# The adaLN map of layer 0 in quarters beside the input projection

## The chip, the cores and the metric

The kernel runs on one core of one Trainium2 chip. The metric is the device time of one execution in microseconds (us); less is better. Times of runs are given as medians; the profile comes from one execution of its own.

## What is computed

Two layers of a hybrid diffusion backbone over 512 latent and 256 context tokens of width 1024. Only the start of layer 0 matters here. Each token stream gets a shift and a scale from a linear map of its conditioning vector (adaLN); the tokens are normalised, modulated, and multiplied by one input weight:

```python
mod_l = [m[:, None, :] for m in jnp.split(jax.nn.silu(c) @ w_m + b_m, 6, axis=-1)]
mod_c = jnp.split(jax.nn.silu(c_ctx) @ w_m + b_m, 6, axis=-1)
zl = modulate(rms_norm(hl, norm1_g[layer]), mod_l[0], mod_l[1])
zc = modulate(rms_norm(hc, norm1_g[layer]), mod_c[0], mod_c[1])
...
h = z @ w_in
qa, ka, va, cq, ckv, kr = jnp.split(h, EVEN_SPLITS, axis=-1)
```

The columns of w_in are 512 for the queries qa, 256 for ka and va, and 416 for the latents cq, ckv and kr. The map w_m is 1024 x 6144; shift and scale are its first 2048 columns.

## The kernel before

**Data.** Tokens stand with features on the partitions: the 1024 features are 8 k tiles of 128 (KT = 8), so `x3[:, k, :]` is one k tile of all 768 tokens, latent tokens in 0:512 and context tokens in 512:768. A modulated k tile is kept as a pair `zs[k]` (high and low part, tiles `sl`), and a weight unit as a pair too (tiles `w`, made by `wunit` from a raw tile `raw` that a DMA fills: L119 on ScalarE casts the high part, L120 on VectorE subtracts). A product takes three matmuls, high by high, high by low, low by high (L295, L297, L298 in `proj`).

**The map.** `mod_steps` returns 9 steps: step k loads the rows of k tile k for the columns that are wanted (L152) and multiplies them into one PSUM bank (L154; four groups of columns, each in its own 32 partitions), and the last step copies the bank (L160), transposes it (L163) and adds the bias, which gives `modT`. For layer 0 the shift and scale columns come as two halves, `start[0]` and `start[1]`; half h serves the k tiles 4h to 4h+3 of z. Each half is 16 DMAs of 256 KB.

**Norm.** `rstd_steps` gives three steps for a range of tokens: squares summed over k, `total` (a matmul by ones, L247, a little work on VectorE at L250 and on GpSimd at L251), and `spread` (a matmul that repeats the result over the partitions, L256). `normed(h, gi)` makes the gain and the k tiles of half h for token group gi (0 latent, 1 context): L274 on VectorE, L277 on ScalarE, L278 on VectorE.

**Projection.** `proj` goes through k tiles and, within one, through token blocks of 128. The accumulators of ka and va for the four latent blocks share two PSUM banks (`on`), those of qa for the four latent blocks are four banks (`tw`), those of qa for the two context blocks two more (`on`). The written order is: for each half, ka/va of the latent blocks, qa of the latent blocks, (after half 0: the z of the rest), qa of the context blocks. Then ka/va of the context blocks, then the latents (416 columns).

**What sets the order.** Each engine runs its queue in order. The queue of TensorE (PE) is set by a scheduler, except inside a `manual_schedule` block, where it is the order in which the code stands; before, only the 9 steps of `start[0]` are such a block, and the scheduler is free to move matmuls of the projection ahead of or between those of `start[1]`. The other engines' queues and that of the DMAs (SP) are the scheduler's. Tiles come from pools: 11 tiles `w` of 1024 columns (WT), 4 tiles `raw` (RAWS), 33 tiles `sl` (SLAB), 4 single PSUM banks `on`. What fills a tile of a pool waits until the tile's earlier user has been read for the last time.

## Time and profile before

| | us |
|---|---|
| median of 3 runs | 1602.92 (1601.92 to 1606.02) |
| the profiled execution | 1602.01 |
| its span in the profile | 1600.2 |

The span runs from the first to the last instruction that the profile shows; 1.8 us of the execution lie around it. PE is TensorE's matmuls, PEld its weight loads, DVE VectorE, ACT ScalarE, POOL GpSimd, SP the queue that issues the DMAs. An fp32 matmul of the program stands in the profile as two records (128 records of L154 for the 64 matmuls of the map).

### The profile page before, as it was taken

The numbers are of one execution on the slowest core, as the hardware profiler recorded it, in microseconds if no ns is written. First come the engines' busy times: TensorE is split into PE (matmuls) and PEld (weight loads), VectorE is DVE, ScalarE is ACT, GpSimd is POOL, SyncE is SP. The second block draws the span as 40 slices with busy tenths as digits, with TensorE's granted clock in tenths as the row PEclk, the third lists the DMA queues.
The fourth block names the chain that finished last, engine by engine and source line by source line (L and its number), as shares of the span: only waits on it lengthen the run. The fifth ranks groups of instructions, "written<-read, shape, count | busy, mean of one in ns | idle before, by whom it ended". The sixth has DMA issues, their size and how long they took to land.

```text
span 1600.2 us, 25191 instructions
## 1 busy us (share of the span) xinstructions
PE 1539.1 (96%) x9394; PEld 1290.4 (81%) x9394; DVE 1106.6 (69%) x1955; ACT 806.1 (50%) x1574; POOL 353.0 (22%) x607
## 2 busy tenths in 40 slices
PE   6998999999999999999999999999999799999996
PEld 3786666658888888888888888778779799999986
DVE  4667765575469967865487557866667788877775
ACT  4447876674334233232331324535666767766663
POOL 0146444440011011010100100122324222222213
PEclk9999999999999999999999999999999899999998
DMA  9410014354123523622254211321134677776651
GB/s 314 158 53 27 1 53 159 106 172 164 54 80 112 158 66 122 208 65 66 66 172 145 63 57 45 108 66 40 40 87 99 146 181 172 165 175 161 167 119 65
DMA packets 81068, 179.19 MB, mean 112 GB/s; under 512 B 9393, under 2 KB 23729, under 8 KB 80945
## 3 DMA queue, kind: packets, MB, share of 16 engines
q1 hardware_dynamic: 67408, 152.93, 30.4%
q0 software_dynamic: 13536, 24.65, 9.0%
q8 instruction: 74, 1.21, 0.3%
q14 instruction: 50, 0.40, 0.1%
HBM read 150.80 MB, written 2.10 MB: 96 GB/s over the span
## 4 chain that ended last, share of the span: by engine, by line
PE 86%; DVE 5%; ACT 3%; issue 2%; DMA 2%; POOL 1%; SPq 0%; DVEq 0%; ACTq 0%; POOLq 0%
PE tw L125 9%; PE tw L126 9%; PE tw L127 9%; PE on L125 8%; PE on L126 7%; PE on L127 7%; PE on L621 3%; PE on L613 2%; PE on L1398 2%; PE on L1399 2%; PE on L1400 2%; PE tw L298 2%; PE tw L295 2%; PE tw L297 2%; PE tw L1398 2%
## 5 line engine op out<-in xcount | busy, mean ns | idle before, releaser
L125 PE MATMUL tw<-sl,w 128*128 128x512 f32 (+1 forms) x832 | 281.9, 339 | 0.1
L126 PE MATMUL tw<-sl,w 128*128 128x512 f32 (+1 forms) x832 | 280.9, 338 | 0.0
L127 PE MATMUL tw<-sl,w 128*128 128x512 f32 (+1 forms) x832 | 280.3, 337 | 0.0
L120 DVE TENSOR_TENSOR w<-raw,w 128x1024 fp32r<-128x1024 f32 (+3 forms) x119 | 137.7, 1159 | 139.8 <-PE tw L126 98.9
L119 ACT CAST w<-raw 128x1024 fp32r<-128x1024 f32 (+3 forms) x119 | 117.4, 990 | 175.3 <-PE tw L127 152.7
L125 PEld LDWEIGHTS tw<-sl,w 128*128 128x128 f32 x832 | 157.1, 189 | 27.4 <-issue 3.6
L125 PE MATMUL on<-sl,w 128*128 128x512 f32 (+2 forms) x504 | 174.0, 346 | 0.0
L126 PEld LDWEIGHTS tw<-sl,w 128*128 128x128 f32 x832 | 157.1, 189 | 18.9 <-issue 0.8
L127 PE MATMUL on<-sl,w 128*128 128x512 f32 (+2 forms) x504 | 171.7, 341 | 0.0
L126 PE MATMUL on<-sl,w 128*128 128x512 f32 (+2 forms) x504 | 171.7, 341 | 0.0
L127 PEld LDWEIGHTS tw<-sl,w 128*128 128x128 f32 x832 | 156.8, 188 | 17.7
L945 POOL TENSOR_SCALAR sm<-sm,csum,cw 128x2 f32<-128x2 f32 x44 | 30.3, 690 | 477.4 <-ACT sm L944 477.4
L1398 PE MATMUL on<-sl,w 128*128 128x256 f32 x384 | 109.8, 286 | 11.0 <-ACT sl L1463 9.9
L572 POOL TENSOR_SCALAR sl<-sl,sm 128x768 f32<-128x768 f32 (+2 forms) x96 | 84.7, 883 | 159.8 <-DVE sm L571 137.6
L125 PEld LDWEIGHTS on<-sl,w 128*128 128x128 f32 x504 | 95.6, 190 | 19.3 <-issue 7.3
L1399 PE MATMUL on<-sl,w 128*128 128x256 f32 x384 | 109.3, 285 | 0.0
L1400 PE MATMUL on<-sl,w 128*128 128x256 f32 x384 | 109.1, 284 | 0.0
L127 PEld LDWEIGHTS on<-sl,w 128*128 128x128 f32 x504 | 95.3, 189 | 11.1
L126 PEld LDWEIGHTS on<-sl,w 128*128 128x128 f32 x504 | 95.7, 190 | 9.8 <-DVE sl L132 0.2
L963 DVE SCALAR_TENSOR_TENSOR sl<-sl,cw,sl 128x770 f32<-128x770 f32 x88 | 89.4, 1019 | 19.6 <-ACT sl L960 17.9
L570 ACT ACTIVATE sl<-tw,sm 128x768 f32<-128x768 f32 (+2 forms) x96 | 81.8, 852 | 40.2 <-DVE sm L569 32.9
L569 DVE TENSOR_REDUCE sm<-tw 128x1 f32<-128x768 f32 (+2 forms) x96 | 84.9, 886 | 18.2 <-PE tw L787 12.0
(318 smaller groups left out, 3829.0 us busy)
## 6 DMA issues: line engine op xcount, KB each, us to landing
raw<-in_ffn_up_w_dram SPq DMA_DIRECT2D x88, 512.0 KB, 3.7
mraw<-in_mod_w_dram SPq DMA_DIRECT2D x96, 256.0 KB, 3.6
raw<-in_mod_w_dram SPq DMA_DIRECT2D x32, 512.0 KB, 4.0
w<-sl POOLq DMA_DIRECT2D x62, 256.0 KB, 4.1
rawd<-in_ffn_down_w_dram SPq DMA_DIRECT2D x48, 192.0 KB, 3.6
sl<-in_mod_w_dram SPq DMA_DIRECT2D x32, 256.0 KB, 5.4
raw<-in_ffn_down_w_dram SPq DMA_DIRECT2D x16, 512.0 KB, 3.6
w<-raw POOLq DMA_DIRECT2D x32, 256.0 KB, 4.4
```

Source lines behind the costliest of these rows:

```text
L119: act.copy(out=h, in_=raw)
L120: dve.tensor_tensor(out=l, in0=raw, in1=bc(h), op=ALU.subtract)
L125: pe.matmul(out=ps, lhsT=lh, rhs=rh, start=first, stop=False)
L126: pe.matmul(out=ps, lhsT=lh, rhs=rl, start=False, stop=False)
L127: pe.matmul(out=ps, lhsT=ll, rhs=rh, start=False, stop=last)
L569: dve.tensor_reduce(out=st[:, 0:1], in_=ps, axis=AX.X, op=ALU.max, negate=True)
L570: act.activation(out=p, in_=ps, func=AF.Exp, bias=st[:, 0:1], accum_out=st[:, 1:2])
L572: pool.tensor_scalar(out=p, in0=p, scalar1=st[:, 2:3], scalar2=1.0, op0=ALU.mult, op1=ALU.mult)
L963: dve.scalar_tensor_tensor(out=r[:, 2:end], in0=h[:, 2 + o:end + o], scalar=cw[:, f, t:t + 1], in1=r[:, 2:end], op0=ALU.mult, op1=ALU.add)
L1398: pe.matmul(out=ps, lhsT=h[:, o], rhs=rh, start=(first and k == 0), stop=False, skip_group_check=True)
L1399: pe.matmul(out=ps, lhsT=h[:, o], rhs=rl, start=False, stop=False, skip_group_check=True)
L1400: pe.matmul(out=ps, lhsT=l[:, o], rhs=rh, start=False, stop=(last and k == 3), skip_group_check=True)
```

## The change

The shift and scale columns of the map come in four quarters, `start[0]` to `start[3]`, of two k tiles of z each. A step is still one k tile of the map, with four column groups, now 128 wide instead of 256. A DMA takes two k tiles at a time (`rows=2`): 256 columns of 128 x 2 rows, so 256 KB as before, in runs of 1 KB instead of 2 KB; a quarter is 8 DMAs. A `manual_schedule` block now also holds the projection of the latent tokens: between the matmuls of quarter q (its two k tiles, each ka/va and then qa) stand the steps of quarter q+1, two at a time, and `normed` makes two k tiles at a time. The context norm's `total` and `spread` and the z of all context k tiles come in the last quarter, and qa of the context blocks after all of the latent tokens' projection. The calls of `wunit` move with it: a weight unit is asked for one quarter ahead. The number of matmuls of the projection stays; the map's matmuls are twice as many at half the width.

```diff
--- before.py
+++ after.py
@@ -137,7 +137,8 @@
 
     modT = [cp.tile([128, 2, 48], F32, name=f"modT{l}") for l in range(2)]
 
-    def mod_steps(layer, c0s, w):
+    def mod_steps(layer, c0s, w, rows=1):
+
 
         M = {}
         run = 2
@@ -147,9 +148,14 @@
             if k == 0:
                 M["ps"] = one()
             for i in range(0, 4, run):
-                raw = raw_tile(1024) if run * w > 512 else slab()
-                src = A["mod_w"][layer, k * 128:(k + 1) * 128, c0s[i]:c0s[i] + run * w]
-                nc.sync.dma_start(out=raw[:, :run * w], in_=src)
+                if k % rows == 0:
+                    n = rows * run * w
+                    raw = raw_tile(1024) if n > 512 else slab()
+                    src = A["mod_w"][layer, k * 128:(k + rows) * 128, c0s[i]:c0s[i] + run * w]
+                    nc.sync.dma_start(out=raw[:, :n].rearrange("p (j c) -> p j c", j=rows),
+                                      in_=src.rearrange("(j p) c -> p j c", j=rows))
+                    M[i] = raw[:, :n].rearrange("p (j c) -> p j c", j=rows)
+                raw = M[i][:, k % rows]
                 for g in range(i, i + run):
                     pe.matmul(out=M["ps"][32 * g:32 * g + 32, :w], lhsT=cT[:, k, :],
                               rhs=raw[:, (g - i) * w:(g - i + 1) * w], start=(k == 0), stop=(k == KT - 1))
@@ -308,7 +314,7 @@
     G2 = [LAT + (0,), CX + (1,)]
     G1 = [LAT + (0,)]
     GH = [(0, 256, 0), (256, 512, 0)]
-    start = [mod_steps(0, [512 * h, 512 * h + 256, 1024 + 512 * h, 1280 + 512 * h], 256) for h in range(2)]
+    start = [mod_steps(0, [256 * q, 256 * q + 128, 1024 + 256 * q, 1152 + 256 * q], 128, 2) for q in range(4)]
     ukv, uqa = {}, {}
     rows = [rstd_steps(x3, a, b) for a, b, _ in G2]
     rsb = slab()
@@ -317,6 +323,14 @@
     def spread(gi):
         a, b, _ = G2[gi]
         act.copy(out=rsb[:, a:b], in_=rows[gi][2]()[:, :b - a])
+
+    g1 = cp.tile([128, 2, KT], F32, name="gain1")
+
+    def normed(q, gi):
+        a, b, s = G2[gi]
+        dve.scalar_tensor_tensor(out=g1[:, s, 2 * q:2 * q + 2], in0=modT[0][:, s, 8 + 2 * q:10 + 2 * q], scalar=1.0,
+                                 in1=ng1[:, 2 * q:2 * q + 2], op0=ALU.add, op1=ALU.mult)
+        norm_mod(x3, 0, 0, g1, [G2[gi]], [rsb[:, a:b]], zs, range(2 * q, 2 * q + 2))
 
 
     with tc.manual_schedule(engines={mybir.EngineType.PE}):
@@ -328,24 +342,39 @@
                 spread(0)
             if i == 5:
                 ukv[0] = wunit(A["ev_w_kv"][0], 1024)
-    for u in range(2):
-        uqa[u] = wunit(A["ev_w_qa"][u], 1024)
-    for k in range(KT):
-        nc.sync.dma_start(out=x3[:, k, SEQ:T], in_=A["x_cols"][:, k, SEQ:T])
-    g1 = cp.tile([128, 2, KT], F32, name="gain1")
-
-    def normed(h, gi):
-        a, b, s = G2[gi]
-        dve.scalar_tensor_tensor(out=g1[:, s, 4 * h:4 * h + 4], in0=modT[0][:, s, 8 + 4 * h:12 + 4 * h], scalar=1.0,
-                                 in1=ng1[:, 4 * h:4 * h + 4], op0=ALU.add, op1=ALU.mult)
-        norm_mod(x3, 0, 0, g1, [G2[gi]], [rsb[:, a:b]], zs, range(4 * h, 4 * h + 4))
-    zs = [(slab(F32R), slab(F32R)) for _ in range(KT)]
-    normed(0, 0)
-    rows[1][0]()
-    rows[1][1]()
-    spread(1)
-    for f in start[1]:
-        f()
+                uqa[0] = wunit(A["ev_w_qa"][0], 1024)
+        zs = [(slab(F32R), slab(F32R)) for _ in range(KT)]
+        normed(0, 0)
+        shared = banks(0, 2)
+        accs = [shared[t // 2][:, (t % 2) * 256:(t % 2) * 256 + 256] for t in range(4)]
+        qacc = banks(2, 0)
+        for q in range(4):
+            steps = start[q + 1] if q < 3 else []
+            for i, kk in enumerate((2 * q, 2 * q + 1)):
+                for f in steps[4 * i:4 * i + 2]:
+                    f()
+                proj(accs, zs, ukv, A["ev_w_kv"], 4, 256, range(4), (kk,), True)
+                for f in steps[4 * i + 2:4 * i + 4]:
+                    f()
+                if i == 0 and q < 3:
+                    uqa[q + 1] = wunit(A["ev_w_qa"][q + 1], 1024)
+                    if q == 0:
+                        ukv[1] = wunit(A["ev_w_kv"][1], 1024)
+                    if q == 1:
+                        for k in range(KT):
+                            nc.sync.dma_start(out=x3[:, k, SEQ:T], in_=A["x_cols"][:, k, SEQ:T])
+                        rows[1][0]()
+                if i == 1 and q < 3:
+                    steps[8]()
+                    normed(q + 1, 0)
+                proj(qacc, zs, uqa, A["ev_w_qa"], 2, 512, range(4), (kk,))
+                if i == 0 and q == 3:
+                    rows[1][1]()
+                    spread(1)
+                    for j in range(4):
+                        normed(j, 1)
+        qacc += banks(0, 2)
+        proj(qacc, zs, uqa, A["ev_w_qa"], 2, 512, (4, 5))
     cosh = const("cos_h", [128, 4 * 64])
     sinh = const("sin_h", [128, 4 * 64])
     cosr = const("cos_r", [128, 4 * 32])
@@ -418,18 +447,6 @@
         act.copy(out=va[:, t], in_=ps[:, 128:256].rearrange("p (h d) -> p h d", d=64))
         qk_norm(krot[t // 3][:, t % 3], k3, 2, t, cgk, sgk, qkg[:, 128:192])
 
-    shared = banks(0, 2)
-    accs = [shared[t // 2][:, (t % 2) * 256:(t % 2) * 256 + 256] for t in range(4)]
-    qacc = banks(2, 2)
-    for h in range(2):
-        ks = range(4 * h, 4 * h + 4)
-        proj(accs, zs, ukv, A["ev_w_kv"], 4, 256, range(4), ks, True)
-        proj(qacc, zs, uqa, A["ev_w_qa"], 2, 512, range(4), ks)
-        if h == 0:
-            normed(0, 1)
-            normed(1, 0)
-            normed(1, 1)
-        proj(qacc, zs, uqa, A["ev_w_qa"], 2, 512, (4, 5), ks)
     for t in range(4):
         gqa_kv(accs[t], t)
     shared = banks(0, 1)[0]
```

The queues that result, at the three places that matter; `on`, `tw` are PSUM banks, the number is that of the tile, `x2` is the number of equal instructions in a row.

PE before, at the end of the first half of the map: the last step, its transpose (`on_211`), and the first matmuls of qa (`tw_406`, weight `w_221`) of k tile 0.

```order
L154 MATMUL on_124<-sl_201,cT 32x256 x2
L154 MATMUL on_124<-sl_205,cT 32x256 x2
L163 MATMUL on_211<-ident,hf_209 128x128 x2
L295 MATMUL tw_406<-w_221,sl_240 128x512
L297 MATMUL tw_406<-w_222,sl_240 128x512
L295 MATMUL tw_407<-w_221,sl_240 128x512
```

PE now, at the end of the first quarter: its transpose (`on_202`), two steps of the second quarter (`on_237`), and only then the first matmuls of the projection (ka/va of k tile 0, `on_233`).

```order
L169 MATMUL on_202<-ident,hf_200 128x128
L160 MATMUL on_237<-sl_238,cT 32x128 x2
L160 MATMUL on_237<-sl_242,cT 32x128 x2
L160 MATMUL on_237<-sl_238,cT 32x128 x2
L160 MATMUL on_237<-sl_242,cT 32x128 x2
L301 MATMUL on_233<-w_178,sl_208 128x256
L303 MATMUL on_233<-w_179,sl_208 128x256
```

So the projection of the first quarter stands behind the second quarter's first two DMAs, `sl_238` and `sl_242`. The same pattern follows eleven times more: one step pair ahead of each ka/va and each qa of the k tiles 0 to 5.

SP before, behind the first half's last DMA: one weight unit, the context tokens, small tables, a weight unit, and the second half.

```order
L152 DMA sl_205<-in_mod_w_dram 128x512
L117 DMA raw_225<-in_ev_w_qa_dram 128x1024
L334 DMA big_69<-in_x_cols_dram 128x256 x8
L85 DMA cos_h_380<-in_cos_h_dram 128x256
...
L117 DMA raw_581<-in_ev_w_kv_dram 128x1024
L152 DMA sl_307<-in_mod_w_dram 128x512
```

SP now, from the first quarter's last DMAs to the second quarter's first two.

```order
L155 DMA sl_188<-in_mod_w_dram 128x2x256
L155 DMA sl_192<-in_mod_w_dram 128x2x256
L117 DMA raw_280<-in_ev_w_kv_dram 128x1024
L117 DMA raw_400<-in_ev_w_qa_dram 128x1024
L365 DMA big_69<-in_x_cols_dram 128x256 x8
L117 DMA raw_551<-in_ev_w_qa_dram 128x1024
L155 DMA sl_238<-in_mod_w_dram 128x2x256
L155 DMA sl_242<-in_mod_w_dram 128x2x256
```

Between the two quarters stand three weight units of 512 KB and the 1 MB of context tokens. `raw_400` reuses the raw tile of the first unit, so it waits for VectorE's L120 of that unit.

SP now, ahead of the fourth quarter (`sl_515`, `sl_519`), with what each waits for.

```order
L1343 DMA rawd_12619<-in_ffn_down_w_dram 128x384 [waits DMAHW0_49]
L117 DMA raw_939<-in_ev_w_lat_dram 128x832 [waits DMAHW1_49,DVE_49,Activation_49]
L155 DMA sl_515<-in_mod_w_dram 128x2x256 [waits DMAHW2_49,PE_49]
L155 DMA sl_519<-in_mod_w_dram 128x2x256 [waits DMAHW3_49,PE_49]
L155 DMA sl_539<-in_mod_w_dram 128x2x256 [waits DMAHW4_49,PE_49]
```

VectorE now, at the same time.

```order
L247 TENSOR_TENSOR hf_414<-hf_414,hf_434 128x256 [waits DVE_49,Activation_49]
L120 TENSOR_TENSOR w_554<-raw_551,w_553 128x1024 [waits DMAHW0_49,PE_49]
L390 SCALAR_TENSOR_TENSOR tabs<-cos_h_779,qk_g_787 128x256 [waits DMAHW1_49,PE_49]
L178 TENSOR_TENSOR modT_94<-on_487,mod_b_cols_78 128x2 [waits PE_49]
L178 TENSOR_TENSOR modT_94<-on_487,mod_b_cols_78 128x2 x3
```

The latent unit `raw_939` takes the raw tile of the fourth qa unit (`raw_551`), so it waits for that unit's L120, which writes `w_554`. That is the twelfth tile `w` in use, and it takes the place of the first ka/va unit's high part, which PE reads for the last time in ka/va of k tile 3. Before, all 16 DMAs of the second half stood ahead of any weight unit that waits for VectorE.

## Rows read from the trace of the kernel before

**Rows 1.** The page: span; busy time, share and instructions by engine.

```profile
span 1600.2 us, 25191 instructions
PE 1539.1 (96%) x9394; PEld 1290.4 (81%) x9394; DVE 1106.6 (69%) x1955; ACT 806.1 (50%) x1574; POOL 353.0 (22%) x607
```

**Rows 2.** Busy time by stage: stretch, length, each engine, PE clock, DMA share, GB/s.

```profile
26.70:49.30 22.60, 19.52 (x121) 13.15 (x122) 13.20 (x31) 8.22 (x17) 0.70 (x1) 0.92 0.95 333
49.30:88.80 39.50, 39.50 (x243) 35.19 (x243) 34.56 (x79) 20.83 (x42) 11.92 (x14) 1.00 0.30 90
88.80:107.10 18.30, 18.30 (x100) 18.06 (x99) 10.43 (x23) 4.40 (x14) 10.30 (x10) 1.00 0.15 44
```

**Rows 3.** The DMA queue in order of time: start, length, line, what.

```profile
5.99 4.84 SPq L152 DMA_DIRECT2D sl<-in_mod_w_dram  x6
...
21.19 5.57 SPq L334 DMA_DIRECT2D big<-in_x_cols_dram  x8
...
30.61 10.52 SPq L152 DMA_DIRECT2D sl<-in_mod_w_dram  x16
```

**Rows 4.** The same view as rows 2, for stretches of the DMA traffic.

```profile
0.00:29.30 29.30, 14.74 (x84) 6.71 (x85) 10.10 (x20) 12.77 (x18) 2.16 (x10) 1.00 0.92 317
25.00:27.00 2.00, 1.20 (x8) 0.35 (x6) 0.30 (x4) 0.93 (x2) 0.00 (x0) 1.00 1.02 348
36.00:39.00 3.00, 3.00 (x15) 2.42 (x14) 2.86 (x7) 0.69 (x1) 0.00 (x0) 1.00 1.05 402
31.00:33.00 2.00, 2.00 (x6) 1.52 (x5) 2.00 (x4) 1.86 (x5) 0.00 (x0) 0.50 0.75 223
```

**Rows 5.** ScalarE in order of time, the first weight units.

```profile
19.12 0.59 ACT L319 COPY sl<-on 128x512 f32<-128x512 f32 x1 [6.83 <-PE on L256]
19.61 1.99 ACT L119 CAST w<-raw 128x1024 fp32r<-128x1024 f32 x2
```

**Rows 6.** VectorE in order of time, the same units.

```profile
20.69 2.36 DVE L120 TENSOR_TENSOR w<-raw,w 128x1024 fp32r<-128x1024 f32 x2 [5.27 <-ACT w L119]
```

**Rows 7.** PE in order of time, the map's second half among qa's matmuls.

```profile
41.80 1.49 PE L154 MATMUL on<-sl,cT 128*32 128x256 f32 x20
43.22 0.50 PE L295 MATMUL tw<-w,sl 128*128 128x512 f32 x1
43.65 0.63 PE L154 MATMUL on<-sl,cT 128*32 128x256 f32 x4
44.21 0.50 PE L297 MATMUL tw<-w,sl 128*128 128x512 f32 x1
44.55 0.40 PE L298 MATMUL tw<-w,sl 128*128 128x512 f32 x1
44.78 0.39 PE L295 MATMUL tw<-w,sl 128*128 128x512 f32 x1
```

**Rows 8.** PE in order of time, end of the map's second half.

```profile
47.85 0.82 PE L154 MATMUL on<-sl,cT 128*32 128x256 f32 x8
49.14 0.44 PE L163 MATMUL on<-ident,hf 128*128 128x128 f32 x2 [0.47 <-ACT hf L160]
49.33 0.37 PE L295 MATMUL on<-w,sl 128*128 128x256 f32 x1
49.54 0.27 PE L297 MATMUL on<-w,sl 128*128 128x256 f32 x1
49.65 0.28 PE L298 MATMUL on<-w,sl 128*128 128x256 f32 x1
```

**Rows 9.** The context norm's step: PE.

```profile
39.43 0.50 PE L247 MATMUL on<-ones,hf 128*128 128x1 f32 x4
```

**Rows 10.** The same step on GpSimd.

```profile
40.21 0.70 POOL L251 TENSOR_TENSOR sm<-sm,mhalf 128x2 f32<-128x2 f32 x1 [23.61 <-DVE sm L250]
```

**Rows 11.** PE in order of time, the wait ahead of the projection.

```profile
28.80 0.50 PE L295 MATMUL tw<-w,sl 128*128 128x512 f32 x1 [2.13 <-ACT sl L277]
```

**Rows 12.** DMA issues from 50 to 60 us: KB each, us from issue to landing.

```profile
raw<-in_ev_w_lat_dram SPq DMA_DIRECT2D x1, 416.0 KB, 3.0
```

## The prediction

> **What bounds the kernel now.** The page first [rows 1]: PE is busy 96% of the span, so a change matters only where it moves PE's dense work. The change lies in the first 110 us, so I read busy time by stage next [rows 2]. Between 26.7 and 49.3 PE is busy on paper (19.5 of 22.6), but the DMA share is 0.95: the stage ends when the map's second half is in. From 49.3 to 88.8, and on to 107.1, PE is busy all the time (39.50 of 39.50, 18.30 of 18.30) and the DMAs are at 0.30 and 0.15. At 88.8 the latents' projection (416 columns) begins, which the change leaves alone. So I ask when PE gets to that point. Later, PE's waits hang on work that follows it (attention's first chain), so I carry a shift at 88.8 to the end unchanged.
>
> The DMA queue [rows 3] shows why: issues follow each other from the start, the first half of the map from 6.0, the context tokens from 21.2, the 16 DMAs of the second half from 30.6 to 41.1. What PE does before 49.3 is a gain that the kernel already has: the scheduler moved the first 48 matmuls of qa (k tiles 0 to 3) into the wait.
>
> **When the new projection can start.** In PE's new queue the first matmul of the projection stands behind the second quarter's first two DMAs, and a queue runs in order. Ahead of and with them the DMA queue now carries 8768 KB: tables 64, latent tokens 2048, first quarter 2048, six weight units 3072, context tokens 1024, the two tiles 512. That is 8.98 MB. Before, the first 29.3 us moved 317 GB/s [rows 4], so they take 28.3 us. Runs of 1 KB are dearer: the context tokens, also 1 KB runs at the same pitch, went at 348 GB/s, the map's 2 KB runs at 402 [rows 4]. For ten tiles (2.62 MB) that is 7.5 instead of 6.5 us, +1.0.
>
> The Trainium skill ("DMA: Bandwidth & Descriptors", Specifications) has transfers reach line rate from 512 B on; by that the +1.0 would be nothing and the sum below 1610.8. The rows differ (348 against 402), and I go by them.
>
> One issue is gated: the third qa unit's raw tile is free when VectorE has subtracted for the first unit. ScalarE casts that one at 19.6, after the norm's copy at 19.12 [rows 5], and VectorE is done with it at 20.69 + 1.18 = 21.9 [rows 6]. By then the units ahead are nearly through, and I put the hole in the traffic at 0.6 (0 to 1.2). [...] Start of the projection: 28.3 + 1.0 + 0.6 + 1.0 = 30.9; bounds 29.3 and 32.5. The z of k tile 0 is ready before that (map of the first quarter in at about 22, then copy, transpose, three weight casts ahead on VectorE, gain, norm: about 28), so it isn't what is waited for.
>
> **What PE has to do from there to 88.8's point.**
>
> Core work, unchanged: the 39.5 us from 49.3 to 88.8 [rows 2], plus the 48 matmuls of qa that now come after the start, at 0.23 each (44.55 to 44.78) [rows 7], 11.2. Together 50.7.
>
> The map between the matmuls, 12 insertions of two k tiles. Before, 20 records (2.5 k tiles of 256 columns) took 1.42 with a switch (41.80 to 43.22), so 0.44 to 0.57 for one [rows 7]. At 128 columns one costs half of that if the columns set it, all of it if the count does. I take the columns, since the time of the projection's matmuls goes with them (0.23 for 512, 0.11 for 256, 49.54 to 49.65 [rows 8]): 0.45 for an insertion; upper bound 1.1. Each insertion also costs two switches between full-width matmuls and the narrow ones: a qa matmul ahead of one took 0.43 (43.22 to 43.65) instead of 0.23, the narrow ones ran 0.1 over, and the next qa matmul took 0.34 (44.21 to 44.55): 0.4 in all [rows 7]. So 0.85 each (0.5 to 1.5), 12 of them, half of the first before the start: 9.8. Before, half of this work lay under the DMA wait, so it cost nothing; that cover is gone, since PE is now the one that is waited for.
>
> Three ends of a quarter. PE's queue has the transpose right behind the last step, so PE waits for ScalarE's copy: before, 48.67 to 49.33, 0.66 [rows 8]. With half the width I take 0.5, times 3: 1.5 (1.0 to 2.0).
>
> The context norm. Its `total` and `spread` now follow each other in PE's queue. From L247's start at 39.43 [rows 9] to GpSimd's end at 40.21 + 0.70 [rows 10] is 1.5; the four records of `spread` 0.5; switches 0.3: 2.3 (1.8 to 2.8). Before, six qa matmuls covered that wait.
>
> The clock. Before, PE waited 2.13 us ahead of 28.80 [rows 11], and then ran at 0.50 of its clock between 31 and 33 [rows 4], 1.2 GHz instead of 2.4; over the stage the granted clock was 0.92 of 22.6 us [rows 2], 1.8 us lost. Then, that loss lay in the DMA wait. Now PE idles from about 23 to 30 and does work that counts afterwards: 1.8 (0.9 to 3.6).
>
> The fourth quarter's DMAs. They stand behind a latent unit whose raw tile is free after L120 of the fourth qa unit, which itself needs PE to have finished ka/va of k tile 3. From that matmul: L120 1.2 with its hand-over 1.3, the latent unit 3.0 from issue to landing [rows 12], two tiles at 348 GB/s 1.5: 5.8. PE meanwhile has an insertion (0.85), the quarter's end (0.5) and qa of k tile 3 (2.8): 4.2. It waits 1.6 (0.5 to 2.5). The third quarter's first tiles come in just ahead of PE by this count: a quarter costs PE some 12 us, and from the second quarter's start to there the queue carries 4.2 MB, 10.4 to 12 us at 402 to 348 GB/s. I put that at nothing (up to 2.0).
>
> Off the path: the context z on VectorE and ScalarE (16 + 16 operations near the end) has qa of k tile 7 and then qa of the context blocks as cover; the evictions of qa start earlier relative to PE than before.
>
> **Sum.** 30.9 + 50.7 + 9.8 + 1.5 + 2.3 + 1.8 + 1.6 = 98.6, against 88.8: 9.8 later. From the profiled execution's 1602.0 (0.9 below the median of the runs): 1611.8, say **1612**. All bounds low: 29.3 + 50.7 + 6.0 + 1.0 + 1.8 + 0.9 + 0.5 = 90.2, 1603.4. All high: 32.5 + 50.7 + 18.0 + 2.0 + 2.8 + 3.6 + 2.5 + 2.0 = 114.1, 1627.
>
> **Rivals.**
>
> *Insertions are cheap.* The narrow matmuls and switches cost 0.5 each, and the start comes a microsecond early: 5 us less, 1606.6, within 0.3% of before (4.8 us, about what a measurement can tell from no change). For it: before, several steps in a row ran close to the columns' rate. Against it: all three switches in rows 7 cost.
>
> *The clock falls again.* The quarter's ends, the fourth quarter's wait and the context norm are waits of 0.5 to 1.6 us each; if two or three of them bring back 1.2 GHz for as long as the one before (1.8 lost each), the time is 1615 to 1617. The Trainium skill ("TensorE: Matmul & The Clock Gate", Loop structure matters more than you think) warns of this loop: a DMA wait between matmuls leaves PE cold. The trace agrees as far as 2.13 us of waiting go (0.50 afterwards); no row above shows it after shorter ones.
>
> *VectorE falls behind.* Context z, four ka/va blocks and the weights of the latents now crowd into the same 20 us, where VectorE was busy 34.56 of 39.50 [rows 2]. If a latent weight is late, 1 to 3 us more: 1614.
>
> *The start is early, and the time falls.* The place is the wait for `sl_238` and `sl_242`. Each microsecond earlier is a microsecond less. At 402 GB/s throughout, 8.98 MB need 22.3 us, landing at about 24.2. With every other term at its low bound, a start before 88.8 - 4.8 - (50.7 + 6.0 + 1.0 + 1.8) = 24.5 makes it faster than before by 0.3%: 1597. Against it: before, the first 29.3 us reached only 317 GB/s, and a gated issue comes on top.
>
> **How the numbers follow.** Forecast 0.58; insertions cheap 0.18; clock 0.15; VectorE 0.05; early start 0.04. Slower by over 0.3%: 0.58 + 0.15 + 0.05 = 0.78; same 0.18; faster 0.04. The range leaves out the early start, the lowest corner of the cheap case, and the far end of the clock case: 1604 to 1620.
>
> **What would show it.** PE's first ka/va matmul at 30 to 32 us, behind a wait for the second quarter's DMA; 0.50 clock around it. Insertions of 0.8 to 0.9 us from matmul to matmul. A gap before the fourth quarter's first narrow matmul, ended by a DMA. A gap of about 1.5 between L253 and L262. The first 416-column matmul at about 98. The prediction is wrong if that matmul comes before 93, if ka/va starts before 28, or if an insertion costs under 0.5; and its last step is wrong if the shift there isn't the shift at the end.

## The result and the profile after

The changed kernel takes 1615.64 us (median of 4 runs, 1614.52 to 1619.2), the kernel before in the same comparison 1602.42: ratio 1.0089, 95% interval 1.0069 to 1.011. It is slower by about 13 us where 10 were forecast, and the time lies in the range. PE's first 416-column matmul, 88.76 before, comes at 101.29 (98.6 forecast); the profiled span grows by 12.5, as much as that matmul moves. The matmul in before:

```profile
88.76 0.35 PE L295 MATMUL tw<-w,sl 128*128 128x416 f32 x1
```

Lines of after: `proj` is L301, L303, L304, the map L160 and its transpose L169, `total` L253, L257 (GpSimd), `spread` L262, the tokens' transposes L515.

The page of after, the same two lines as in [rows 1]:

```profile
span 1612.7 us, 25466 instructions
PE 1539.5 (95%) x9522; PEld 1295.8 (80%) x9522; DVE 1107.6 (69%) x1967; ACT 806.3 (50%) x1576; POOL 356.9 (22%) x607
```

PE is as busy as before (1539.5 against 1539.1) in a span 12.5 longer, so the loss shows as idle time. Where PE waits between 20 and 125, by the view of waits of after (who on which line, for what; us in total, times, longest):

```profile
PE on L160 <- DMA sl<-in_mod_w_dram: 11.6, 4, 9.6
PE on L515 <- DVE sl L438: 2.4, 2, 1.4
PE on L169 <- ACT hf L166: 1.8, 4, 0.5
```

With a wait of 1.03 for GpSimd at L262 that is 16.8 us, where before has 5.2 by the same view. 11.6 of it is the map's own DMAs, and one wait of 9.6 leads. Busy time by stretch of after (columns as in [rows 2]) shows what the DMAs did around it:

```profile
0.00:22.00 22.00, 8.41 (x72) 5.75 (x76) 6.14 (x10) 10.19 (x15) 2.16 (x10) 1.00 0.85 288
22.00:24.00 2.00, 0.87 (x13) 0.41 (x13) 2.00 (x3) 1.91 (x3) 0.00 (x0) 1.00 0.38 82
24.00:33.00 9.00, 0.06 (x2) 0.09 (x4) 5.92 (x13) 3.25 (x5) 0.00 (x0) 0.53 0.91 307
33.00:38.10 5.10, 5.10 (x44) 3.93 (x44) 0.00 (x0) 0.21 (x1) 0.00 (x0) 0.50 1.03 342
```

In 22 to 24 the queue ran dry: 82 GB/s. The reason stands in the DMA queue of after in order of time (start, length of the group's issues, line, what), and in one row of VectorE:

```profile
15.56 0.54 SPq L117 DMA_DIRECT2D raw<-in_ev_w_kv_dram  x1
22.23 0.34 SPq L117 DMA_DIRECT2D raw<-in_ev_w_qa_dram  x1
22.61 3.75 SPq L365 DMA_DIRECT2D big<-in_x_cols_dram  x8
...
26.88 5.65 SPq L155 DMA_DIRECT2D sl<-in_mod_w_dram  x8
...
56.85 0.33 SPq L117 DMA_DIRECT2D raw<-in_ev_w_lat_dram  x1
57.30 4.43 SPq L155 DMA_DIRECT2D sl<-in_mod_w_dram  x8
```

```profile
20.97 3.50 DVE L120 TENSOR_TENSOR w<-raw,w 128x1024 fp32r<-128x1024 f32 x3 [4.91 <-ACT w L119]
```

Behind the issue at 15.56 nothing is issued until 22.23: the third qa unit wants the raw tile that the first of VectorE's three subtractions frees, and the context tokens, another unit and the second quarter stand behind it. The same once more with the latent unit at 56.85, ahead of the fourth quarter; the issue before it ends at 48.49.

PE of after in order of time (wait ahead of a group in brackets), at the places of the sum:

```profile
32.94 1.70 PE L160 MATMUL on<-sl,cT 128*32 128x128 f32 x16 [9.56 <-DMA sl<-in_mod_w_dram]
34.58 0.58 PE L301 MATMUL on<-w,sl 128*128 128x256 f32 x1
...
37.44 0.97 PE L160 MATMUL on<-sl,cT 128*32 128x128 f32 x16
...
41.02 0.40 PE L304 MATMUL tw<-w,sl 128*128 128x512 f32 x1
41.34 0.64 PE L160 MATMUL on<-sl,cT 128*32 128x128 f32 x16
41.92 0.39 PE L301 MATMUL on<-w,sl 128*128 128x256 f32 x1
42.14 0.28 PE L303 MATMUL on<-w,sl 128*128 128x256 f32 x1
...
43.32 0.28 PE L304 MATMUL on<-w,sl 128*128 128x256 f32 x1
...
44.70 0.48 PE L301 MATMUL tw<-w,sl 128*128 128x512 f32 x1
...
59.31 0.40 PE L304 MATMUL tw<-w,sl 128*128 128x512 f32 x1
61.11 0.41 PE L160 MATMUL on<-sl,cT 128*32 128x128 f32 x4 [1.40 <-DMA sl<-in_mod_w_dram]
61.83 0.63 PE L160 MATMUL on<-sl,cT 128*32 128x128 f32 x12 [0.30 <-DMA sl<-in_mod_w_dram]
62.39 0.39 PE L301 MATMUL on<-w,sl 128*128 128x256 f32 x1
...
77.95 0.39 PE L304 MATMUL tw<-w,sl 128*128 128x512 f32 x1
...
79.71 0.71 PE L262 MATMUL on<-ident,sm 128*128 128x128 f32 x4 [1.03 <-POOL sm L257]
80.18 0.36 PE L301 MATMUL on<-w,sl 128*128 128x256 f32 x1
...
101.29 0.35 PE L301 MATMUL tw<-w,sl 128*128 128x416 f32 x1
```

How to read off an insertion: between two qa matmuls lie 0.23, between two ka/va matmuls 0.12. From 41.02 to 41.92 there are 0.90, so the sixteen records cost 0.67; the next ka/va follows after 0.22 instead of 0.12: 0.77 in all. In the same way a quarter's end costs 44.70 - 43.32 - 0.12 - 0.67 = 0.6 beside its insertion; the fourth quarter's wait 62.39 - 59.31 - 0.23 - 0.67 = 2.2; the context norm 80.18 - 77.95 - 0.23 = 2.0. At half clock ka/va takes 2.86 (34.58 to 37.44) instead of 1.61 (41.92 to 43.53), the insertion behind it 0.90 instead of 0.57: 1.6.

### The profile page after: what moved, and what is told of

The parts are those of the page before. It is cut to its first block, busy times and chain, and to the rows that moved or that the text cites. A ratio compares the mean times of both kernels' runs of the same rounds, so it can differ in the third digit from the quotient of the medians.

```text
span 1612.7 us, 25466 instructions
## 1 busy us (share of the span) xinstructions
PE 1539.5 (95%) x9522; PEld 1295.8 (80%) x9522; DVE 1107.6 (69%) x1967; ACT 806.3 (50%) x1576; POOL 356.9 (22%) x607
## 4 chain that ended last, share of the span: by engine, by line
PE 86%; DVE 5%; ACT 3%; issue 2%; POOL 2%; DMA 2%; SPq 0%; DVEq 0%; POOLq 0%; ACTq 0%
PE tw L125 9%; PE tw L127 9%; PE tw L126 9%; PE on L125 7%; PE on L126 7%; PE on L127 7%; PE on L638 3%; PE on L630 2%; PE on L1415 2%; PE on L1416 2%; PE on L1417 2%; PE tw L301 2%; PE tw L304 2%; PE tw L1415 2%; PE tw L303 2%
## 5 line engine op out<-in xcount | busy, mean ns | idle before, releaser
L120 DVE TENSOR_TENSOR w<-raw,w 128x1024 fp32r<-128x1024 f32 (+3 forms) x119 | 137.6, 1159 | 143.6 <-PE tw L126 94.6
```

Of the source, the lines that this page charges most:

```text
L120: dve.tensor_tensor(out=l, in0=raw, in1=bc(h), op=ALU.subtract)
```

## The experiments

The theory: the change loses time because PE now waits in order for the map's DMAs, and each term of the sum is lost by itself. Rivals: the terms hide one another, because the DMA queue is the bound in any case; or the narrow matmuls and the switches to and from them are what costs. The table has all runs; "at" is PE's first 416-column matmul in the profile, and times are medians of n runs beside the kernel before (1602.1 to 1602.9).

| kernel | at | us (n) | ratio to before |
|---|---|---|---|
| before | 88.76 | 1602.42 (4) | |
| after | 101.29 | 1615.64 (4) | 1.0089 [1.0069, 1.011] |
| k tile 0 first | 102.03 | 1611.82 (4) | 1.0054 [1.0038, 1.0071] |
| queue as written | 93.01 | 1605.2 (10) | 1.0018 [1.0008, 1.0029] |
| extra matmuls | 103.36 | 1613.16 (1) | |
| long runs | 100.96 | 1610.42 (1) | |
| total early | 101.88 | 1618.31 (1) | |
| queue by hand | 93.44 | 1607.8 (9) | 1.0027 [1.0015, 1.0038] |
| one insertion | 88.62 | 1599.97 (1) | |
| one insertion, total early | 86.58 | 1598.63 (12) | 0.9974 [0.9963, 0.9986] |
| before, queue as written | 100.44 | 1615.11 (6) | 1.0073 [1.0056, 1.0091] |
| ScalarE, VectorE as written | 86.48 | 1604.01 (1) | |
| ka/va first | 87.51 | 1596.06 (1) | |
| both | 86.99 | 1601.99 (12) | 0.9984 [0.9969, 0.9998] |

A single time says little here: runs of one kernel lie up to 10 us apart. The matmul's place is the finer reading, but it comes from one profiled execution of each kernel; how far it moves from run to run isn't shown.

**K tile 0 first.** The products of k tile 0 go ahead of the second quarter's first four steps.

```diff
-                for f in steps[4 * i:4 * i + 2]:
-                    f()
+                if kk:
+                    for f in steps[4 * i:4 * i + 2]:
+                        f()
...
                 proj(qacc, zs, uqa, A["ev_w_qa"], 2, 512, range(4), (kk,))
+                if kk == 0:
+                    for f in steps[0:4]:
+                        f()
```

> All that moves is PE's order: the products of k tile 0 (ka/va and qa) stand ahead of the second quarter's first four steps instead of behind two of them. The reading is PE's first 416-column matmul (before 88.76, after 101.29). Theory of the prediction (the start of the projection is bound by the wait for the second quarter's tiles, and a shift there is a shift of the end): ka/va of k tile 0 starts when VectorE has its low half, 28.1 in the profile after, instead of 34.58; the narrow matmuls find their tiles landed; the 416-column matmul comes 4 to 5 us earlier, 96.3 to 97.3, and the time is about 1611. Rival, the clock takes it: the early products run at 1.2 GHz as long as the late ones did or longer, and only 1 to 3 us are left. Rival, the DMA queue is the bound in any order: the next tiles or weights are late instead, and the matmul stays within 1 us of 101.3.

PE's ka/va starts at 25.46, nine us earlier than after, and the 416-column matmul comes at 102.03, not earlier at all. The second rival came true (the DMA queue is the bound in any order); the first one's sign is there too, 0.50 clock from 24 to 30.7. PE in order of time, at the start, the third and the fourth quarter:

```profile
25.46 0.58 PE L301 MATMUL on<-w,sl 128*128 128x256 f32 x1 [3.09 <-ACT sl L283]
...
43.86 0.41 PE L160 MATMUL on<-sl,cT 128*32 128x128 f32 x4 [2.28 <-DMA sl<-in_mod_w_dram]
...
59.27 0.41 PE L160 MATMUL on<-sl,cT 128*32 128x128 f32 x4 [1.19 <-DMA sl<-in_mod_w_dram]
```

PE is early and waits at the next gate; the projection's DMA waits come to 5.5 us with the smaller ones (0.33 twice, and 1.41). Behind each of the two the clock falls again, here by stretch behind the second:

```profile
61.50:64.80 3.30, 3.30 (x22) 2.80 (x20) 0.00 (x0) 0.00 (x0) 0.00 (x0) 0.50 0.72 247
```

So a shift of the start is no shift of the 416-column matmul while a later DMA wait stands behind it.

**Extra matmuls.** Ten idle float32 matmuls fill PE's wait.

```diff
+        warm = one()
+        for _ in range(10):
+            pe.matmul(out=warm, lhsT=ident, rhs=x3[:, 0, 0:512], start=True, stop=True)
+        act.copy(out=wt, in_=warm[:, 0:1])
         normed(0, 0)
```

> Ten extra matmuls of 512 columns (float32, into a bank that nothing uses) fill PE's idle time behind the first quarter's end, 23.4 to about 32; they compute nothing that the output needs. Theory of the prediction (the clock falls because PE waits, and the half clock from there to 38.16 costs 2.6 us): the granted clock stays at 2.4 GHz or is back at it by 33, and the 416-column matmul comes 2 to 3 us earlier, 98.3 to 99.3. Rival, the clock falls for another reason than PE's idle time, or such matmuls don't hold it up: the clock is at 1.2 GHz all the same, the ten take 17 us instead of 8.5, and the matmul comes at 101 or, pushed by them, up to 8 us later.

By stretch:

```profile
24.00:31.00 7.00, 7.00 (x18) 3.04 (x16) 5.20 (x9) 2.29 (x3) 0.00 (x0) 1.00 0.89 284
```

And PE in order of time at the third and fourth quarter:

```profile
47.28 0.41 PE L160 MATMUL on<-sl,cT 128*32 128x128 f32 x4 [1.57 <-DMA sl<-in_mod_w_dram]
...
61.63 0.41 PE L160 MATMUL on<-sl,cT 128*32 128x128 f32 x4 [1.60 <-DMA sl<-in_mod_w_dram]
```

The clock stays at 1.00 (2.4 GHz) where it had fallen to 0.50 (1.2 GHz): its fall in after comes from PE's idle time, as the prediction had it. But the time won is lost again at the third quarter, where after had no wait, and at the fourth, behind which the clock falls after all (0.50 in 63.5 to 66.9): 103.36. The mechanism held, the price did not: the clock's 1.6 us were worth nothing here.

**Long runs.** Runs of 2 KB instead of 1 KB for the map.

```diff
-                    src = A["mod_w"][layer, k * 128:(k + rows) * 128, c0s[i]:c0s[i] + run * w]
-                    nc.sync.dma_start(out=raw[:, :n].rearrange("p (j c) -> p j c", j=rows),
-                                      in_=src.rearrange("(j p) c -> p j c", j=rows))
+                    src = A["mod_w"][layer, k * 128:(k + 1) * 128, c0s[i]:c0s[i] + n]
+                    nc.sync.dma_start(out=raw[:, :n], in_=src)
```

> Each DMA of the map reads one row of 512 neighbouring columns (runs of 2 KB) instead of two rows of 256 (1 KB): the same bytes into the same tile, but other columns of the map than the kernel needs, so its values are not the reference's; nothing else changes. Theory (1 KB runs cost what the rows showed, 348 against 402 GB/s): a tile of 256 KB takes 0.65 instead of 0.75 us, so the tile that ended the first wait lands about 1.0 earlier than 33.53, and the 416-column matmul comes about 1.0 earlier, 100.3; the fourth quarter's wait shrinks by 0.2. Rival (runs of 1 KB move as fast as those of 2 KB, and the wait is made by the number of bytes and the gated issue): the tile lands within 0.3 of 33.53 and the matmul stays at 101.3. The Trainium skill (DMA: Bandwidth & Descriptors, Specifications) has line rate from 512 B on, by which the rival holds.

By stretch, first with the map's tiles in flight, then behind them:

```profile
17.00:19.00 2.00, 2.00 (x16) 1.76 (x19) 0.00 (x0) 0.19 (x1) 0.00 (x0) 1.00 1.06 406
20.00:22.50 2.50, 0.66 (x21) 0.39 (x13) 2.13 (x2) 2.50 (x5) 0.00 (x0) 1.00 0.10 41
```

The runs do move faster, 406 GB/s where after had 377 (17 to 20), and 402 against 372 at 33 to 35. Yet PE's wait ends only 0.16 earlier (32.78), and the 416-column matmul 0.33. The first half of the theory held, the second fell: what is won ahead of the gated issue only makes the hole in the traffic longer (41 GB/s for 2.5 us). The fourth quarter's waits came to 2.03 (1.06 and 0.97) instead of 1.70, where 0.2 less was expected. The Trainium skill (DMA: Bandwidth & Descriptors, Specifications) has line rate from 512 B on. The rates don't bear that out (377 GB/s against 406), though the kernel's time comes out nearly as by that rule, for another reason.

**Queue as written.** PE's order stays; the DMA queue keeps the order of the code.

```diff
-    with tc.manual_schedule(engines={mybir.EngineType.PE}):
+    with tc.manual_schedule(engines={mybir.EngineType.PE, mybir.EngineType.SP}):
```

> PE's order is as after; SP's queue over the projection keeps the order in which the code is written, so the second quarter's tiles come ahead of two weight units, the third and fourth qa units and the context tokens (about 6.6 MB ahead of and with them instead of 8.98), and no latent unit stands ahead of the fourth quarter. Theory: the first narrow matmul starts at 28 to 29 (the tiles are in at 22 to 24, and PE then waits for z of k tile 0 at 28.1), 4 to 5 us earlier, and the fourth quarter's wait of 1.7 is gone: the 416-column matmul at 94 to 96, the time about 1609 to 1610. Rival, weights late instead: the fourth qa unit or the context tokens come late behind the tiles, a wait of 1 to 4 us takes the place, and the matmul comes at 98 to 101. Rival, the wait was not the bound: it stays at 101.

The waits up to 88:

```profile
PE on L160 <- DMA sl<-in_mod_w_dram: 3.2, 2, 3.0
```

And ka/va of k tile 0, the second of its matmuls (28.56 the first), and the first 416-column matmul, in order of time:

```profile
28.94 0.42 PE L303 MATMUL on<-w,sl 128*128 128x256 f32 x1
...
93.01 0.35 PE L301 MATMUL tw<-w,sl 128*128 128x416 f32 x1
```

One name in that list of engines moves the matmul from 101.29 to 93.01, more than the theory gave it. The 9.6 are gone and so is the fourth quarter's wait; what is left of DMA waits is 3.0 ahead of the first quarter's own tiles. (The profile shows no clock below 1.00 here, since its clock records begin at 31.59; the durations of 0.42, 0.28 at full clock, say that this ka/va of k tile 0 still ran at half.) So three terms of the sum, the start, the fourth quarter and part of the clock, were one thing: which bytes stand ahead of which in one queue.

**Total early.** `total` ahead of qa of k tile 6, `spread` behind it.

```diff
-                proj(qacc, zs, uqa, A["ev_w_qa"], 2, 512, range(4), (kk,))
                 if i == 0 and q == 3:
                     rows[1][1]()
+                proj(qacc, zs, uqa, A["ev_w_qa"], 2, 512, range(4), (kk,))
+                if i == 0 and q == 3:
                     spread(1)
```

> As after, but the context norm's total stands ahead of qa of k tile 6 and its spread behind it, so that 24 matmuls cover the way over VectorE and GpSimd. Theory: PE's wait of 1.03 ahead of the spread (78.67 to 79.71) goes and nothing takes its place, and the first 416-column matmul comes 1.0 to 1.3 earlier than 101.29: 100.0 to 100.3. Rival: the end hangs on something else there (the context z behind it on VectorE), and PE waits as long at the context blocks: 101.3.

The wait for GpSimd is gone from the list of waits, but the matmul comes at 101.88. The fourth quarter's waits were longer in this profile (1.53 and 0.59), and the clock fell behind them. By stretch:

```profile
62.30:65.60 3.30, 3.30 (x24) 2.89 (x16) 0.00 (x0) 0.00 (x0) 0.00 (x0) 0.50 0.93 314
```

Taken by itself the run does not show the gain; 3.3 us at half clock cost about 1.7 and the longer wait 0.3 (its second group of narrow matmuls starts at 62.13 instead of 61.83), so some 1.4 were gained there, which is worked out, not shown. In the step from 88.62 to 86.58 below the same wait of 1.03 goes and none takes its place, but of that step of 2.04, 0.66 is an earlier start and 0.81 a wait at a transpose; only some 0.6 is left for it.

**Queue by hand, and one insertion.** The DMAs are taken out of the steps and issued in the order of use, each quarter one ahead: first quarter, two units, second quarter, two units, third quarter, and so on. Then, on top of it, the steps of a quarter in one piece.

```diff
+        for k in range(0, KT, 2):
+            start[0][9](k)
+        ukv[0] = wunit(A["ev_w_kv"][0], 1024)
+        uqa[0] = wunit(A["ev_w_qa"][0], 1024)
+        for k in range(0, KT, 2):
+            start[1][9](k)
...
+                if i == 1 and q < 3:
+                    steps[8]()
+                    normed(q + 1, 0)
                 proj(accs, zs, ukv, A["ev_w_kv"], 4, 256, range(4), (kk,), True)
+                if i == 0:
+                    for f in steps[0:8]:
+                        f()
```

> The insertions as after; the DMA queue is written by hand: all eight tiles of the first quarter, then one ka/va and one qa unit, the second quarter, the two units of the next k tiles, the third quarter, and so on, each quarter one ahead of its use. The run before showed PE waiting for the first quarter's own tiles (20.66 to 23.70), with two weight units and the tables among them. Theory (the order of bytes sets the start): the first quarter is in at about 17 instead of 23.7, some 5.5 us of copy, transpose, gain and norm follow, ka/va of k tile 0 starts at 23 to 24 instead of 28.56, no DMA wait comes after it, and the 416-column matmul at 87.5 to 89 instead of 93.0; time about 1600. Rival, the latents' norm or VectorE's weights bound the start: 26 to 27, and the matmul at 91. Rival, the total of bytes bounds again: waits of 1 to 3 us for the second or third quarter, matmul at 90 to 92.

The queue by hand moves 359 and 378 GB/s (20 to 24, 24 to 31) and leaves no DMA wait, and ka/va starts at 25.92 (23 to 24 expected): the first rival, not the queue, was next. The matmul stays at 93.44, because a new wait came that nobody had named. ScalarE in order of time:

```profile
46.15 2.97 ACT L246 ACTIVATE hf<-big 128x256 f32<-128x256 f32 x8 [6.24 <-DMA big<-in_x_cols_dram]
```

PE's transpose that waits for the copy behind them:

```profile
49.37 0.33 PE L173 MATMUL on<-ident,hf 128*128 128x128 f32 x1 [1.80 <-ACT hf L170]
```

The squares of the context tokens, now late in the queue, stand ahead of the map's copy on ScalarE (49.05); PE waits 1.80, where such a wait was 0.44 in after, and then runs 3.3 us at half clock, 1.7 lost: 3.1 in all, more than the 2.6 by which ka/va starts earlier than with the queue as written.

> The queue by hand as in the run beside it, but the eight steps of a quarter come as one insertion between ka/va and qa of the quarter's first k tile, and the transpose ahead of ka/va of the second: 3 insertions of 32 narrow matmuls instead of 12 of 8, and qa covers ScalarE's copy. Theory (an insertion of 0.77 is about half switches): 9 pairs of switches at 0.3 to 0.4 and three quarter ends at 0.5 are saved, 4 to 5 us: 416-column matmul at 83 to 85. Rival (the narrow matmuls themselves cost it): one insertion takes 4 x 0.77 = 3.1, only the quarter ends are saved, 1.0 to 1.5. Rival: the second quarter's tiles, now needed earlier, are waited for: 1 to 2 us at the first insertion.

88.62, not 83 to 85: it starts from 93.44 instead of 88, and the step is 4.8 against 4 to 5 expected. That the step agrees is in part luck: the insertions behind ka/va's start give 2.2 (eleven of 0.77 against three of 2.08, below), and the transposes' waits (0.81 instead of 2.68) and the half clock that is gone there (1.7) give more than the forecast had for the quarter ends, while ka/va starts 0.7 later (26.61). PE in order of time, one insertion:

```profile
51.96 0.28 PE L308 MATMUL on<-w,sl 128*128 128x256 f32 x1
52.17 1.95 PE L164 MATMUL on<-sl,cT 128*32 128x128 f32 x64
54.06 0.50 PE L305 MATMUL tw<-w,sl 128*128 128x512 f32 x1
```

64 records cost 54.06 - 51.96 - 0.12, and 0.10 for the next qa matmul (at 54.39): 2.08, where four insertions of 16 cost 3.08. With c for the records of two steps and s for a pair of switches, c + s = 0.77 and 4c + s = 2.08: c = 0.44, s = 0.33. The theory's half was a little too much, and the prediction's 0.45 for the columns was right to 0.01.

> The queue by hand, one insertion for each quarter, and the context norm's total ahead of qa of k tile 6. Theory (the terms add, and a shift of the 416-column matmul is a shift of the end but for what the clock does later): 1.0 less than the run beside it, 82 to 84, that is 5 to 7 earlier than the kernel before, and the time 1596 to 1599, ratio to before 0.996 to 0.998. Rival (what PE gains there is lost behind VectorE, which follows it up to the transposes): the matmul comes early, the end does not, ratio 0.999 to 1.001.

The 416-column matmul at 86.58, the ratio 0.9974 [0.9963, 0.9986]: a version that beats both kernels, though the matmul is 2 us, not 5 to 7, ahead of the kernel before. So the expected ratio (0.996 to 0.998) came out, but not by the way that the theory gave. Behind VectorE's waits of 2.4 us at the transposes the lead is down to 0.27 (PE's next matmuls, L708, start at 111.23, those of before, L681, at 111.50): there the rival held. What the profile gains at the end, 7.0 us, it gains later; among other things it shows full clock around 450 us, where before ran at half clock (below). The gain is measured; what makes it is not shown.

What is left at the start: ScalarE has the latents' norm copy (L329) at 22.93, behind two casts (21.04, 1.99 long), and VectorE the first z (L284) at 24.40, behind their two subtractions.

**Before, queue as written.** Is the gain the queue's alone?

```diff
+    with tc.manual_schedule(engines={both[1]}):
...
+        for f in start[1]:
+            f()
+        ukv[0] = wunit(A["ev_w_kv"][0], 1024)
+        for k in range(KT):
+            nc.sync.dma_start(out=x3[:, k, SEQ:T], in_=A["x_cols"][:, k, SEQ:T])
```

> The kernel before (the map in halves, no quarters), with its DMA queue over the start in written order: the second half's tiles come ahead of the context tokens, of one ka/va unit and of two others. This asks whether the gain of the best version so far is the queue's or the quarters'. Theory (the queue alone would have helped the kernel before as well, since its stage up to 49.3 is a DMA stage): about 1.2 MB less ahead of the second half's end, 3 to 4 us, so the first 416-column matmul at 85 to 86 instead of 88.76, as good as the quarters with the same care (86.58), time 1597 to 1600. Rival (the slabs of the first half or the latents' qa work bound the second half, not the bytes): 88 to 89, and then the quarters are what gains 2 us.

PE in order of time, from the end of the second half on:

```profile
49.21 0.44 PE L163 MATMUL on<-ident,hf 128*128 128x128 f32 x2 [0.53 <-ACT hf L160]
56.01 0.98 PE L247 MATMUL on<-ones,hf 128*128 128x1 f32 x4 [6.37 <-DVE hf L241]
58.95 1.22 PE L256 MATMUL on<-ident,sm 128*128 128x128 f32 x4 [1.96 <-POOL sm L251]
```

The issues of the second half end 3.7 us earlier (26.65 to 37.44 against 41.13 in [rows 3]), but its transpose comes at 49.21, no earlier than in [rows 8]. PE was busy 16.88 of the 17.40 us from 31.8 to there, with qa and the map. So with halves the queue's order gains nothing by that point, and the rival held there. What follows is a loss of the run's own: PE's queue has the context norm's `total` ahead of ka/va, and the context tokens now come late, 6.37 and 1.96 of waiting. PE runs at half clock there (0.50 from 53 to 62), and ka/va starts at 59.83, 10.5 later than in [rows 8]. Its 100.44 is that loss, and what another place for `total` would give was not tried. So whether the queue alone would have helped the kernel before at the end stays open.

**ScalarE and VectorE.** Both engines in written order; ka/va of k tiles 6 and 7 together; both edits.

```diff
-    with tc.manual_schedule(engines={mybir.EngineType.PE, mybir.EngineType.SP}):
+    with tc.manual_schedule(engines={mybir.EngineType.PE, mybir.EngineType.SP, mybir.EngineType.Activation,
+                                     mybir.EngineType.DVE}):
...
-                proj(accs, zs, ukv, A["ev_w_kv"], 4, 256, range(4), (kk,), True)
+                if q < 3 or i == 0:
+                    proj(accs, zs, ukv, A["ev_w_kv"], 4, 256, range(4), (kk,) if q < 3 else (6, 7), True)
```

> The version with the queue by hand, one insertion and the early total; now ScalarE and VectorE also keep the written order over the projection (latents' norm copy and the first two weight units ahead of the map's copy; z of k tile 0 ahead of later weights), and the squares of the context tokens come after the third quarter's norm. In the run before, ScalarE had that norm copy at 22.93 behind two casts, and VectorE its first z at 24.40 behind two weight subtractions, though the map was there at 21.9. Theory: ka/va of k tile 0 starts at 23.3 to 23.8 instead of 25.95, and the 416-column matmul 2 us earlier, 84 to 85. Rival: the second quarter's tiles or units are then late (they landed up to 27.2), and a wait of 1 to 2 takes the place.

> The same best version, but ka/va of k tile 7 stands ahead of qa of k tile 6, so that VectorE can begin with ka/va's four blocks 2.8 us earlier relative to PE. The reading is PE's waits for VectorE among the first transposes behind the latents' projection (0.94 and 1.42 in the version without it, 0.99 and 1.43 after; before 1.05 alone and later). Theory (VectorE is late because ka/va's end stands only 14 us ahead of the 416-column matmul, where it stood 17 ahead before): both waits shrink by 2 us or more in sum, and the transposes' end comes 1.5 to 2.4 earlier relative to the 416-column matmul. Rival (VectorE waits there for GpSimd's small steps, not for its start): the sum of the waits stays over 2.0. The 416-column matmul itself stays within 0.5 of 86.6.

> Both edits of the two runs beside it on the best version. Theory (they add): 416-column matmul at 84 to 85, the transposes' waits under 1 us in sum, time 1594 to 1596, ratio to before 0.995 to 0.997. Rival (the waits only move, as at the context norm): ratio 0.997 to 0.999, as the version without them had.

PE's waits between 88 and 125 (view of waits), in the version without these edits:

```profile
PE on L525 <- DVE sl L448: 2.4, 2, 1.4
```

The same wait with both engines in written order:

```profile
PE on L533 <- DVE sl L456: 4.4, 2, 3.5
```

And with ka/va first:

```profile
PE on L526 <- DVE sl L449: 1.8, 2, 1.4
```

Written order brings ka/va to 25.29, 0.66 earlier instead of 2 to 2.6: VectorE still subtracts both units (20.93 to 23.29) ahead of the map's gain. And VectorE, which then waits for ScalarE between the steps of each z (0.58 and 0.79), ends later than before: 4.4. The 2 us did not come, and neither theory had the later loss. With ka/va of k tile 7 earlier by 2.8, the waits shrink by 0.6 only (and the matmul itself moves by 0.9, where at most 0.5 was expected): the theory (at least 2) falls, and the rival (over 2.0 left) misses by 0.2. In the version without the edits VectorE works from 66.17 to 106 with few gaps, the longest 1.61 behind GpSimd's small steps, and had idled 3.61 ahead of 66.17, until the context norm was spread; so it may be the context norm's place that makes it late, which was not tried. Both edits together give 0.9984 [0.9969, 0.9998], in the rival's range, and waits of 3.4 where under 1 was expected: nothing over the version without them.

## Why the prediction was right, and where it was off

**What bounds, and the reading point.** Right in the medians: the loss is there by the 416-column matmul, 12.53, or 0.78%, inside the interval of the ratio. That the span grows by the same 12.5 is luck. "I carry a shift at 88.8 to the end unchanged" isn't what the traces show behind that point. The shift is 14.5 at PE's first matmuls behind the transposes (L681 at 111.50, L698 of after at 126.05), 10.5 at 816 us (VectorE's L1248 at 815.66, L1265 of after at 826.20), 11.0 at 1032 us and 13.5 at 1089 us (ScalarE's L1034 and L1101, first at 1032.0 and 1088.8; L1051 and L1118 of after at 1043.0 and 1102.3). Much of it is the clock: around 450 us PE of before runs 6.8 us at 0.50, 3.4 lost, and after doesn't; at 1086 us after does, and before doesn't. The stretch of before, then that of after:

```profile
450.00:456.80 6.80, 6.80 (x25) 5.83 (x26) 2.85 (x7) 2.68 (x7) 2.07 (x9) 0.50 0.34 110
462.00:468.80 6.80, 5.25 (x33) 4.16 (x32) 3.57 (x8) 2.85 (x7) 4.00 (x10) 1.00 0.50 154
```

Of the seven versions with an interval, six have the ratio that the matmul's shift gives: after 0.78% against 0.89, queue as written 0.27 against 0.18, queue by hand 0.29 against 0.27, the best -0.14 against -0.26 (at the end of its interval), the kernel before with another queue 0.73 against 0.73, both edits -0.11 against -0.16. "K tile 0 first" would be 0.83 and has 0.54 [0.38, 0.71], with a profiled span that says 0.79. Its four runs had a mean granted clock of 0.984 to 0.988, those of after 0.981 to 0.984, and within a kernel the time goes with that clock ("both": 1595.87 us at 0.989, 1603.38 at 0.982); that this is the difference is likely, not shown. One reading fails: that the stage before 49.3 "ends when the map's second half is in". With those tiles issued 3.7 earlier (before, queue as written) its transpose came at 49.21 all the same, and PE was busy 16.88 of the 17.40 us ahead of it. The sum doesn't use this reading, since it counts from 88.8.

**The start** is the term that was mis-sized. Forecast for the second tile 30.9, so ka/va at 31.3; measured 34.58, 3.3 later and outside the 30 to 32 that the text gave. The step that failed is "I put the hole in the traffic at 0.6", and that all 8.98 MB were divided by one rate. The gate itself was forecast well (21.9, issued 22.23). But a queue that is dry at the gate starts anew: 22.23, plus the 3.0 from issue to landing [rows 12], plus the 2560 KB that stand from the gate to the second tile, 2.62 MB at 317 GB/s = 8.3: 33.5, and PE's matmuls on that tile end at 34.58. That this sum comes out is partly luck: the 3.0 holds a transfer of 416 KB, which the 8.3 counts again. In after the gated unit lands 3.5 behind its issue, at 25.75, and the 2.10 MB behind it take 7.8 us to the second tile's landing at 33.53, only 270 GB/s. What stands ahead of the gate doesn't enter, which is why long runs gained little, and the 1.0 for 1 KB runs was no cost by itself. The last 1.0 of the start's sum (30.9) no run shows: the first tile lands at 32.81 (26.88 + 5.93), and PE's matmuls on it start at 32.94. So the second tile's landing was missed by 3.6 (29.9 by the sum), and PE, which waits less behind it, by 3.3.

**The rest of the way**, from ka/va's start to the 416-column matmul, was forecast as 67.3 and took 66.7:

| term | forecast | measured |
|---|---|---|
| core (12 x 0.12 and 12 x 0.23 for each of 8 k tiles, and the context blocks) | 50.7 | 50.5 |
| 11 insertions | 9.4 | 8.5 (0.77 each) |
| three quarter ends | 1.5 | 1.8 |
| context norm | 2.3 | 2.0 |
| clock | 1.8 | 1.6 |
| fourth quarter's DMAs | 1.6 | 2.2 |

No wait came at the third quarter, as forecast. Of an insertion the columns were right (0.44 for 0.45), the switches 0.33 instead of 0.4.

**What the sum hid.** The terms add up for this kernel, but they are not prices: start nine us earlier, or a clock that doesn't fall, and the matmul stays where it was. The sentence "Each microsecond earlier is a microsecond less" is wrong as long as a later quarter's tiles are gated; the text had them "just ahead of PE", which says that a gain of 2 would find the next wall. Of the single edits to after only the queue's order moved it far, by 8.3. The rival that the narrow matmuls and switches cost it holds for a part: 8.5 us for the eleven insertions, which one insertion a quarter cuts to some 6.2.

**The rivals.** Insertions at 0.5: no, 0.77. The clock falling again: not in after up to the 416-column matmul (no 0.50 behind the 1.40 and 0.30 of the fourth quarter), but in "k tile 0 first", "extra matmuls" and "total early", behind waits only a little longer there. The Trainium skill (TensorE: Matmul & The Clock Gate, Loop structure matters more than you think) warns of a long DMA wait between matmuls. These variants agree where the waits were long (0.50 behind DMA waits of 2.28 and 0.33); behind 1.57 and 0.23 the clock stayed at 1.00. VectorE falling behind: it came true as well, 2.4 us of waits at the transposes (120 to 123) where before had 1.0, and the shift there is 14.5. Behind these waits after runs at 0.50 from 123.5 to 126.9; that the shift is 12.5 again at the end is the coming and going of the clock told above. The early start: no.

## What to carry to other kernels

When a change makes an engine wait in order for a DMA queue, find the last gated issue ahead of what it waits for, and count from there: gate, landing, and only the bytes behind it, at the rate of a queue that starts anew (270 GB/s here). Before adding up terms, ask of each what the next wait behind it would be if it were gone; terms that end at the same queue are one term. And when a split looks too dear, try the order of the queue and the size of the pieces before giving up the split: here the same quarters were 13 us slower than the kernel before, and 4 us faster with the queue by hand, one insertion a quarter and an early `total`. Which of these, or the quarters themselves, makes it faster than before isn't shown. And a forecast from one place to the end needs the clock behind that place: a half-clock stretch of 6.8 us came or went with no edit there, 3.4 us each.

## What the hardware showed unexpectedly

- A queue that has run dry also moved less behind its hole: 307 GB/s in 24 to 33, where the queue by hand, never dry, moved 378 in 24 to 31. The issues there, at 0.47 us each for 128 KB of context tokens (8 in 3.75 us), bring at most 280 GB/s, which may be why; it wasn't tried by itself.
- PE's granted clock fell to 0.50 behind waits of 1.80 (queue by hand), of 2.28 and 0.33, and of 1.19 and 1.41 (k tile 0 first), of 1.60 and 0.43 (extra matmuls) and of 1.53 and 0.59 (total early), but not behind 1.40 and 0.30 (after), 1.57 and 0.23 (extra matmuls) or 1.06 and 0.97 (long runs). Where it fell, 3.3 us at half clock cost 1.7.
- Moving from full-width matmuls to the map's, which write 32 partitions each, and back costs 0.33 a pair here (worked out from two sizes of insertion), nearly three of ka/va's matmuls.
